# The first stage of a two-layer decoder step: input in nine loads, a padded short block, a bank of its own for the norms, and two column pairs side by side

## The chip, the cores and the metric

The kernel runs on one core of a Trainium2 chip. The metric is device time in microseconds (us). The kernel before was timed in three runs: 2272.81, 2275.51 and 2279.55, so its median is 2275.51 us. Engines are named as in the profile: PE is the matrix engine, PEld its weight loads, DVE the vector engine, ACT the scalar engine, POOL GpSimd, and SP the engine that issues most DMAs.

## What is computed

The program is one inference step of a decoder trunk with two layers: an RWKV-7 layer, then a sliding-window attention layer. All of the change lies at the start of the first layer. There the rows of the input are normalised, mixed with the row before, and multiplied by four weight matrices of 2048 x 4096:

```python
hp = concatenate([meta_tokens (16 rows), x_prompt (256 rows)])      # and x_sample: 8 rows
xn = hp * rsqrt(mean(hp * hp, axis=-1) + 1e-6) * a_norm             # D_MODEL = 2048
prev = concatenate([shift_prev, xn[:-1]])                           # state_shift for the samples
xm[p] = xn + (prev - xn) * mu[p]                                    # p = r, k, v, z, w, a
r, k, v, z = xm[p] @ w_rkvz[p]                                      # 2048 x 4096 each
```

The rest (the recurrence over the rows, the output projection and the attention layer) is not touched.

## The kernel before, in words

**Rows and blocks.** The 280 rows (16 meta tokens, 256 prompt rows, 8 samples) and the 8 rows of `state_shift` lie in three blocks `xt[0]`, `xt[1]`, `xt[2]` of 128, 128 and 32 rows by 2048 columns. They come in halves of 1024 columns. The loads of `xt[1]` and of the meta tokens are issued on ACT's queue, the others on SP's (lines 317 to 322). Each engine works through its queue in order, DMA issues included.

**Parameters.** `params` (line 251) is a generator. Its first part loads three small rows of parameters (`a_norm`, `a_mu`, `kv_norm`, lines 256 to 258, on ACT's queue), transposes them on PE into the PSUM bank `ps_par` (line 263) and copies them to `par` (line 264). Its second part does the same with two more blocks of rows, in the same bank.

**Norms.** The squares of each half and block are summed over the columns: block 0 on DVE (line 336), blocks 1 and 2 on ACT (line 334). Twelve small DVE instructions then make `rs`, the inverse root (lines 338, 339 and 299 to 303). Three transposes on PE spread `rs` over the partitions into the bank `ps_rs` (line 343), and ACT copies it to `rsb` (line 346). `ps_par` and `ps_rs` come from the pool `pp`, which has one bank.

**Transposes of the input.** For each of the 16 column blocks k (128 columns), PE transposes the three row blocks into one bank (line 362), and ACT copies the bank to `xn[:, k]` (line 364). The banks rotate over the pools `pe` (two banks), `pc` and `py` (one each). After every fourth k, `xn` is stored (line 366).

**Mixing.** For every group g of two column blocks, DVE multiplies by the norms (line 376), takes differences (lines 378, 379) and makes the mixed input `mst` (line 383). For the keys (m = 1) this runs for g = 0 to 7 in program order; the list of the results is `tk`. There are eight `mst` buffers.

**The keys' product.** `proj` (line 477) makes the result of a pair of 128 columns: it calls a product function, copies the two results (line 487), sums the squares of the keys (lines 490 and 493, bank `ps_kk`) and stores them. For the first two pairs the product function is `gemm32` (line 228): it multiplies in fp32, directly from `tk` and the raw weights. A raw tile holds two column blocks k by 256 columns (256 KB) and there are four such buffers (line 235). A pair needs eight raw tiles, and every fp32 product appears in the trace as two instructions (line 238). Its two result banks come from `pm`, which has three. Between the first and the second pair the program splits the mixed keys into two parts of lower precision, `xk` (cast on ACT, line 186; difference on DVE, line 187; store by SP, line 394), and does the same for five groups of the mixed values (`xv`).

All later products (the other fourteen pairs of the keys, and all of the values, receptance and gate) go through `gemm` (line 212): weights are split into `whi` and `wlo` (lines 186, 187), and each product is three PE instructions (lines 208 to 210). In the two pair-steps after the first two, groups of the mixed values and the mixed gate input are made and split beside the products; `behind` ties them to the weights' splits.

**What sets the order.** The program is written as a flow of data; a scheduler at build time orders the instructions of each engine. It takes them in program order, and lets later ones go first while earlier ones wait for data or buffers by its own estimate of times. Only the mixing for `tk` is bound by hand to its order on DVE.

Of the kernel before, what the change touches and what calls it, by code (L numbers as in the profile page):

```python
# [10 lines left out]
F32 = mybir.dt.float32  # L11
# [14 lines left out]
N = L + NS  # L26
NX = N + NS
NB = SEQ + NS
KT = D // 128
# [83 lines left out]
class Kernel:  # L113
# [113 lines left out]

    def gemm32(self, w, name, nk, col, x):

        ps = [self.bank(self.pm, f"ps_{name}_{col}_{c}") for c in (0, 128)]  # L230
        wv = w.rearrange("(kt p) c -> p kt c", p=128)
        for k0 in range(0, nk, 2):
            raw = self.wp.tile([128, 512], F32, tag="raw", bufs=4, name=f"raw_{name}_{col}_{k0}").rearrange(
                "p (k c) -> p k c", k=2)
            self.nc.sync.dma_start(raw, wv[:, k0:k0 + 2, col:col + 256])
            for i in range(2):
                for k in range(2):
                    self.nc.tensor.matmul(ps[i][:, :N], raw[:, k, 128 * i:128 * i + 128], x(k0 + k),
                                          start=k0 + k == 0, stop=k0 + k == nk - 1)
        return [p[:, :N] for p in ps]  # L240
# [10 lines left out]
    def params(self):  # L251
        nc, I = self.nc, self.I
        v = lambda n, k: I[n].rearrange("o (k c) -> (o k) c", c=128)
        rows = [self.ph.tile([128, 128], F32, name=f"prow{i}") for i in range(3)]

        nc.scalar.dma_start(rows[0][0:16], v('a_norm', 16))
        nc.scalar.dma_start(rows[0][16:112], I['a_mu'].rearrange("o m (k c) -> (o m k) c", c=128))
        nc.scalar.dma_start(rows[0][112:128], I['kv_norm'].rearrange("(k c) -> k c", c=128))
        self.par = self.cp.tile([128, 384], F32, name="par")
        ps = self.bank(self.pp, "ps_par")  # L260
        def par_of(i):
# [4 lines left out]
        yield  # L266
        dma = nc.sync.dma_start
        dma(self.ct[:, 128:], I['consts'][:, 128:C_TOTA])
# [40 lines left out]
    def phase0(self):  # L309
        nc, I, O, ph = self.nc, self.I, self.O, self.ph  # L310
        rows = [128, 128, 32]
        xt = [ph.tile([128, D], F32, name=f"xt{i}") for i in range(3)]
        xp = I['x_prompt'][0]
        dma = nc.sync.dma_start
        halves = slice(0, D // 2), slice(D // 2, D)
        for h in halves:
            nc.scalar.dma_start(xt[1][:, h], xp[112:240, h])
            dma(xt[0][16:128, h], xp[0:112, h])
            dma(xt[2][0:16, h], xp[240:256, h])
            dma(xt[2][16:24, h], I['x_sample'].rearrange("b o d -> (b o) d")[:, h])  # L320
            dma(xt[2][24:32, h], I['state_shift'][0, :, h])
            nc.scalar.dma_start(xt[0][0:16, h], I['meta_tokens'][:, h])
        params = self.params()
# [6 lines left out]
        for c, h in enumerate(halves):  # L330
            for i, r in enumerate(rows):
                sq = ph.tile([128, D // 2], F32, tag=f"sq{i % 2}", name=f"sq0_{i}{c}")[:r]
                if i:
                    nc.scalar.activation(sq, xt[i][:r, h], AF.Square, accum_out=sc[:r, c, i:i + 1])
                else:
                    nc.vector.tensor_tensor_reduce(sq, xt[i][:r, h], xt[i][:r, h], 1.0, 0.0, op0=ALU.mult,
                                                   op1=ALU.add, accum_out=sc[:r, c, i:i + 1])
# [3 lines left out]
        psr = self.bank(self.pp, "ps_rs")  # L341
        for i, r in enumerate((128, 128, 24)):
            nc.tensor.transpose(psr[:, i * 128:i * 128 + r], rs[:r, i:i + 1].to_broadcast((r, 128)),
                                self.ident[:r, :r])
        rsb = ph.tile([128, N], F32, name="rsb")
# [13 lines left out]
        for k in range(KT):  # L359
            ps = self.bank((self.pe, self.pc, self.pe, self.py)[k % 4], f"ps_xn{k}")  # L360
            for i, r in enumerate(rows):
                nc.tensor.transpose(ps[:, i * 128:i * 128 + r], xt[i][:r, k * 128:k * 128 + 128],
                                    self.ident[:r, :r])
            nc.scalar.copy(xn[:, k], ps[:, :NX])
            if k % 4 == 3:
                dma(self.xd[k - 3:k + 1].rearrange("k p t -> p k t"), xn[:, k - 3:k + 1, :N])
# [20 lines left out]
        def part(m, g, tile, t=None):  # L387

            if t is None:
                t = raw_part(m, g)  # L390
            hl = tile(f"d{m}_{g}")
            self.split(hl[:, 0], hl[:, 1], t)
            if m < 4:
                dma(self.md[m][g], hl.bitcast(F32))
            return hl
# [1374 lines left out]
```

## Time and profile before

| what | value |
|---|---|
| median of the three runs | 2275.51 us |
| span of the profiled execution | 2277.2 us |
| instructions | 57029 |
| bytes moved | 455.54 MB, mean 200 GB/s |
| first fp32 product of the keys (L238) | 28.98 us |
| first split product (L208) | 68.97 us |

The profile states the profiled execution's time as its span, from the first to the last instruction; the execution lies between the lowest and the highest of the three runs. All durations in the prediction are from this execution. The views used are: the page (busy time and share of each engine, the chain of work that ended last); busy time by windows (per engine, with the share of time in which the 16 DMA engines were busy, and GB/s); the chain of waits in order of time; the timeline, where each row gives start, length, engine, line and operation, output <- inputs, count, and in brackets the idle time before with what ended it; and groups of instructions, where the numbers are busy time, mean ns of one, and idle time before with what ended it.

### The profile page before, as it was taken

Reading aid. Unit: us, or ns where it says so; the run is one execution under the profiler, and the core shown is the slowest. Engines: PE = TensorE matmul, PEld = TensorE weight load, DVE = VectorE, ACT = ScalarE, POOL = GpSimd, SP = SyncE. Lnnn points to the kernel's source line nnn. Section 1 sums busy time; section 2 is a strip of 40 time slices with the busy share of each in tenths; the row PEclk is TensorE's granted clock in tenths of the full one; section 3 lists DMA queues with packets and bytes.
Section 4 is the critical chain, followed back from the end, with each engine's and each line's share of the span. In section 5 each row is a group of like instructions: output and inputs, shape, how many; then the busy total and the mean of one; then the engine's idle time right before and its main releaser. Section 6 shows DMA issues by size and latency. Waiting matters only on the chain.

```text
span 2277.2 us, 57029 instructions
## 1 busy us (share of the span) xinstructions
PE 2195.4 (96%) x21840; PEld 2029.5 (89%) x21840; DVE 1724.2 (76%) x4168; ACT 1303.8 (57%) x3074; POOL 60.7 (3%) x81
## 2 busy tenths in 40 slices
PE   6999999999999999999999999999999999999997
PEld 4898888899898889889889989999888899899997
DVE  5866756787787768788878878877767777787786
ACT  3556756576666567666665445644545544545443
POOL 0010000000000000000100001100000000000000
PEclk9999999999999999999999999999999999999998
DMA  7978667658755865766647677766434444367774
GB/s 241 340 255 249 185 198 241 194 174 266 227 163 179 247 230 177 246 206 200 201 129 265 192 236 245 227 201 191 134 104 127 133 144 133 105 194 218 232 230 145
DMA packets 424690, 455.54 MB, mean 200 GB/s; under 512 B 64201, under 2 KB 383113, under 8 KB 424025
## 3 DMA queue, kind: packets, MB, share of 16 engines
q1 hardware_dynamic: 423600, 449.61, 63.2%
q8 instruction: 171, 2.80, 0.5%
q10 hardware_dynamic: 816, 2.29, 0.3%
q14 instruction: 103, 0.84, 0.1%
HBM read 385.19 MB, written 70.73 MB: 200 GB/s over the span
## 4 chain that ended last, share of the span: by engine, by line
PE 80%; DMA 7%; DVE 6%; ACT 3%; issue 2%; SPq 0%; POOL 0%; DVEq 0%; ACTq 0%; POOLq 0%
PE ps_z L208 5%; PE ps_z L210 5%; PE ps_z L209 5%; PE ps_q L208 3%; PE ps_q L210 3%; PE ps_v L208 3%; PE ps_q L209 3%; PE ps_ob L210 3%; PE ps_k L208 3%; PE ps_ob L209 3%; PE ps_ob L208 3%; PE ps_v L209 2%; PE ps_v L210 2%; PE ps_k L209 2%; PE ps_k L210 2%; PE ps_r L208 2%
## 5 line engine op out<-in xcount | busy, mean ns | idle before, releaser
L187 DVE TENSOR_TENSOR wlo_z<-raw_z,whi_z 128x512 fp32r<-128x512 f32 x256 | 174.2, 689 | 61.7 <-ACT whi_z L186 54.7
L186 ACT CAST whi_z<-raw_z 128x512 fp32r<-128x512 f32 x256 | 155.8, 618 | 111.8 <-PE ps_z L209 67.9
L208 PE MATMUL ps_z<-mhlm,whi_z 128*128 128x280 f32 x512 | 159.1, 311 | 0.0
L210 PE MATMUL ps_z<-mhlm,wlo_z 128*128 128x280 f32 x512 | 150.3, 294 | 0.7 <-DVE wlo_z L187 0.6
L209 PE MATMUL ps_z<-mhlm,whi_z 128*128 128x280 f32 x512 | 150.0, 293 | 0.0
L208 PE MATMUL ps_q<-bmh,whi_q 128*128 128x264 f32 x512 | 148.5, 291 | 0.0
L208 PE MATMUL ps_z<-bmh,whi_z 128*128 128x264 f32 x512 | 147.4, 290 | 0.0
L209 PE MATMUL ps_q<-bml,whi_q 128*128 128x264 f32 x512 | 147.2, 289 | 0.0
L210 PE MATMUL ps_ob<-ghi,wlo_ob 128*128 128x264 f32 x512 | 145.3, 285 | 1.9 <-DVE wlo_ob L187 1.9
L209 PE MATMUL ps_z<-bml,whi_z 128*128 128x264 f32 x512 | 146.9, 289 | 0.0
L210 PE MATMUL ps_q<-bmh,wlo_q 128*128 128x264 f32 x512 | 146.5, 290 | 0.0
L210 PE MATMUL ps_z<-bmh,wlo_z 128*128 128x264 f32 x512 | 146.4, 289 | 0.0
L208 PE MATMUL ps_ob<-ghi,whi_ob 128*128 128x264 f32 x512 | 144.9, 284 | 0.0
L209 PE MATMUL ps_ob<-glo,whi_ob 128*128 128x264 f32 x512 | 144.7, 283 | 0.1
L187 DVE TENSOR_TENSOR wlo_r<-raw_r,whi_r 128x512 fp32r<-128x512 f32 x128 | 86.9, 686 | 57.2 <-ACT whi_r L186 56.1
L186 ACT CAST whi_oa<-raw_oa 128x512 fp32r<-128x512 f32 x128 | 78.4, 620 | 89.4 <-DMA raw_oa<-a_w_out 32.0
L186 ACT CAST whi_q<-raw_q 128x512 fp32r<-128x512 f32 x128 | 78.9, 621 | 81.6 <-PE ps_q L209 59.6
L187 DVE TENSOR_TENSOR wlo_v<-raw_v,whi_v 128x512 fp32r<-128x512 f32 x128 | 87.4, 688 | 49.5 <-ACT whi_v L186 43.6
L186 ACT CAST whi_ob<-raw_ob 128x512 fp32r<-128x512 f32 x128 | 78.9, 620 | 78.3 <-PE ps_ob L209 61.4
L208 PE MATMUL ps_v<-mhlm,whi_v 128*128 128x280 f32 x384 | 121.8, 317 | 0.2 <-ACT st L743 0.2
L208 PE MATMUL ps_k<-mhlm,whi_k 128*128 128x280 f32 x384 | 119.6, 312 | 0.0
L187 DVE TENSOR_TENSOR wlo_k<-raw_k,whi_k 128x512 fp32r<-128x512 f32 x112 | 76.5, 690 | 53.7 <-ACT whi_k L186 53.0
(486 smaller groups left out, 7686.0 us busy)
## 6 DMA issues: line engine op xcount, KB each, us to landing
raw_k<-a_w_rkvz SPq DMA_DIRECT2D x128, 256.0 KB
raw_v<-a_w_rkvz SPq DMA_DIRECT2D x128, 256.0 KB
raw_r<-a_w_rkvz SPq DMA_DIRECT2D x128, 256.0 KB
raw_z<-a_w_rkvz SPq DMA_DIRECT2D x128, 256.0 KB
raw_oa<-a_w_out SPq DMA_DIRECT2D x128, 256.0 KB
raw_q<-b_w_qz SPq DMA_DIRECT2D x128, 256.0 KB
raw_z<-b_w_qz SPq DMA_DIRECT2D x128, 256.0 KB
raw_ob<-b_w_o SPq DMA_DIRECT2D x128, 256.0 KB
```

Source lines behind the costliest of these rows:

```text
L186: self.nc.scalar.copy(hi, src)
L187: return self.nc.vector.tensor_tensor(lo, src, hi.bitcast(F32), op=ALU.subtract)
L208: mm(ps, wh, xh, start=start, stop=False)
L209: mm(ps, wh, xl, start=False, stop=False)
L210: return mm(ps, wl, xh, start=False, stop=stop)
```

## The change

Five things change, all at the start.

1. The input comes in eight loads, with the load of the constants nine: the meta tokens, the last prompt rows, the samples and `state_shift` come whole instead of in halves; `state_shift` goes to ACT's queue. The three first parameter rows go to SP's queue.
2. The short block `xt[2]` is padded: its rows 32 to 127 are set to zero by two fills on POOL, and its transposes, like the third one of the norms, are 128 x 128.
3. The squares of block 2 move from ACT to DVE.
4. `ps_par` moves to the pool `pc`, so `ps_rs` alone is in `pp` at that time. The transposes of the input now rotate over three banks (`pe`, `pe`, `py`).
5. `gemm32` takes both column pairs at once: per group of two column blocks it loads a raw tile for each pair and multiplies both; the four result banks come from `pm`, `pm`, `pc` and `pp`. The splits of `xk` and `xv` follow in the program after both pairs have been taken through `proj`.

```diff
-    def gemm32(self, w, name, nk, col, x):
+    def gemm32(self, w, name, nk, cols, x):
-        ps = [self.bank(self.pm, f"ps_{name}_{col}_{c}") for c in (0, 128)]
+        pools = self.pm, self.pm, self.pc, self.pp
+        ps = [self.bank(p, f"ps_{name}_{cols[i // 2]}_{i % 2}") for i, p in enumerate(pools)]
         wv = w.rearrange("(kt p) c -> p kt c", p=128)
         for k0 in range(0, nk, 2):
-            raw = self.wp.tile([128, 512], F32, tag="raw", bufs=4, name=f"raw_{name}_{col}_{k0}").rearrange(
-                "p (k c) -> p k c", k=2)
-            self.nc.sync.dma_start(raw, wv[:, k0:k0 + 2, col:col + 256])
-            for i in range(2):
+            for c, col in enumerate(cols):
+                raw = self.wp.tile([128, 512], F32, tag="raw", bufs=4, name=f"raw_{name}_{col}_{k0}").rearrange(
+                    "p (k c) -> p k c", k=2)
+                self.nc.sync.dma_start(raw, wv[:, k0:k0 + 2, col:col + 256])
                 for k in range(2):
-                    self.nc.tensor.matmul(ps[i][:, :N], raw[:, k, 128 * i:128 * i + 128], x(k0 + k),
-                                          start=k0 + k == 0, stop=k0 + k == nk - 1)
+                    for i in range(2):
+                        self.nc.tensor.matmul(ps[2 * c + i][:, :N], raw[:, k, 128 * i:128 * i + 128], x(k0 + k),
+                                              start=k0 + k == 0, stop=k0 + k == nk - 1)
...
-        nc.scalar.dma_start(rows[0][0:16], v('a_norm', 16))
-        nc.scalar.dma_start(rows[0][16:112], I['a_mu'].rearrange("o m (k c) -> (o m k) c", c=128))
-        nc.scalar.dma_start(rows[0][112:128], I['kv_norm'].rearrange("(k c) -> k c", c=128))
+        dma = nc.sync.dma_start
+        dma(rows[0][0:16], v('a_norm', 16))
+        dma(rows[0][16:112], I['a_mu'].rearrange("o m (k c) -> (o m k) c", c=128))
+        dma(rows[0][112:128], I['kv_norm'].rearrange("(k c) -> k c", c=128))
-        ps = self.bank(self.pp, "ps_par")
+        ps = self.bank(self.pc, "ps_par")
...
-        for h in halves:
-            nc.scalar.dma_start(xt[1][:, h], xp[112:240, h])
+        late = nc.scalar.dma_start
+        for c, h in enumerate(halves):
+            late(xt[1][:, h], xp[112:240, h])
             dma(xt[0][16:128, h], xp[0:112, h])
-            dma(xt[2][0:16, h], xp[240:256, h])
-            dma(xt[2][16:24, h], I['x_sample'].rearrange("b o d -> (b o) d")[:, h])
-            dma(xt[2][24:32, h], I['state_shift'][0, :, h])
-            nc.scalar.dma_start(xt[0][0:16, h], I['meta_tokens'][:, h])
+            if c == 0:
+                late(xt[0][0:16], I['meta_tokens'])
+                dma(xt[2][0:16], xp[240:256])
+        dma(xt[2][16:24], I['x_sample'].rearrange("b o d -> (b o) d"))
+        late(xt[2][24:32], I['state_shift'][0])
+        for r in (slice(32, 64), slice(64, 128)):
+            nc.gpsimd.memset(xt[2][r], 0.0)
...
-                if i:
+                if i == 1:
                     nc.scalar.activation(sq, xt[i][:r, h], AF.Square, accum_out=sc[:r, c, i:i + 1])
...
-            nc.tensor.transpose(psr[:, i * 128:i * 128 + r], rs[:r, i:i + 1].to_broadcast((r, 128)),
-                                self.ident[:r, :r])
+            nc.tensor.transpose(psr[:, i * 128:i * 128 + 128], rs[:, i:i + 1].to_broadcast((128, 128)), self.ident)
...
-            ps = self.bank((self.pe, self.pc, self.pe, self.py)[k % 4], f"ps_xn{k}")
+            ps = self.bank((self.pe, self.pe, self.py)[k % 3], f"ps_xn{k}")
-                nc.tensor.transpose(ps[:, i * 128:i * 128 + r], xt[i][:r, k * 128:k * 128 + 128],
-                                    self.ident[:r, :r])
+                nc.tensor.transpose(ps[:, i * 128:i * 128 + 128], xt[i][:, k * 128:k * 128 + 128], self.ident)
...
+        first = self.gemm32(I['a_w_rkvz'][0, 1], "k", KT, (0, 256), lambda k: tk[k // 2][:, k % 2])
         for p0 in (0, 2):
-            self.proj(1, lambda k: tk[k // 2][:, k % 2], [p0], self.kd, self.gemm32)
-            if p0 == 0:
-                xk = [part(1, g, self.mix_tile, tk[g]) for g in range(8)]
-                xv = [part(2, g, lambda nm: mv[g]) for g in range(5)]
+            self.proj(1, None, [p0], self.kd, lambda *_: first[p0:p0 + 2])
+        xk = [part(1, g, self.mix_tile, tk[g]) for g in range(8)]
+        xv = [part(2, g, lambda nm: mv[g]) for g in range(5)]
```

More of the change, by code (lines that the diff above doesn't have):

```diff
@@ L266, in params @@
         yield
-        dma = nc.sync.dma_start
         dma(self.ct[:, 128:], I['consts'][:, 128:C_TOTA])
@@ L310, in phase0 @@
         nc, I, O, ph = self.nc, self.I, self.O, self.ph
-        rows = [128, 128, 32]
         xt = [ph.tile([128, D], F32, name=f"xt{i}") for i in range(3)]
@@ L330, in phase0 @@
         for c, h in enumerate(halves):
-            for i, r in enumerate(rows):
+            for i, r in ((0, 128), (1, 128), (2, 32)):
                 sq = ph.tile([128, D // 2], F32, tag=f"sq{i % 2}", name=f"sq0_{i}{c}")[:r]
-                if i:
+                if i == 1:
                     nc.scalar.activation(sq, xt[i][:r, h], AF.Square, accum_out=sc[:r, c, i:i + 1])
@@ L341, in phase0 @@
         psr = self.bank(self.pp, "ps_rs")
-        for i, r in enumerate((128, 128, 24)):
-            nc.tensor.transpose(psr[:, i * 128:i * 128 + r], rs[:r, i:i + 1].to_broadcast((r, 128)),
-                                self.ident[:r, :r])
+        for i in range(3):
+            nc.tensor.transpose(psr[:, i * 128:i * 128 + 128], rs[:, i:i + 1].to_broadcast((128, 128)), self.ident)
         rsb = ph.tile([128, N], F32, name="rsb")
@@ L359, in phase0 @@
         for k in range(KT):
-            ps = self.bank((self.pe, self.pc, self.pe, self.py)[k % 4], f"ps_xn{k}")
-            for i, r in enumerate(rows):
-                nc.tensor.transpose(ps[:, i * 128:i * 128 + r], xt[i][:r, k * 128:k * 128 + 128],
-                                    self.ident[:r, :r])
+            ps = self.bank((self.pe, self.pe, self.py)[k % 3], f"ps_xn{k}")
+            for i in range(3):
+                nc.tensor.transpose(ps[:, i * 128:i * 128 + 128], xt[i][:, k * 128:k * 128 + 128], self.ident)
             nc.scalar.copy(xn[:, k], ps[:, :NX])
```

## The prediction

> **What bounds the kernel now.** The page is read first: its busy shares and the chain of work that ended last.
>
> ```profile
> PE 2195.4 (96%) x21840; PEld 2029.5 (89%) x21840; DVE 1724.2 (76%) x4168; ACT 1303.8 (57%) x3074; POOL 60.7 (3%) x81
> PE 80%; DMA 7%; DVE 6%; ACT 3%; issue 2%; SPq 0%; POOL 0%; DVEq 0%; ACTq 0%; POOLq 0%
> ```
>
> TensorE (PE) carries the kernel, so a change in the first stage is worth the time by which PE's later products move forward. The next view is busy time by stretches, cut where the first stage changes character.
>
> ```profile
> core 0: us, PE busy (x) PEld busy (x) DVE busy (x) ACT busy (x) POOL busy (x), PEclk, DMA share, GB/s
> 0.00:26.50 26.50, 14.66 (x54) 8.70 (x54) 4.60 (x21) 12.02 (x29) 1.18 (x8) 1.00 0.70 197
> 26.50:53.30 26.80, 20.25 (x71) 14.34 (x72) 25.67 (x57) 5.29 (x10) 0.00 (x0) 1.00 0.87 283
> 53.30:69.00 15.70, 15.45 (x63) 10.60 (x61) 8.12 (x17) 5.54 (x11) 0.00 (x0) 1.00 0.88 310
> 69.00:98.40 29.40, 29.14 (x205) 25.99 (x206) 27.36 (x53) 18.51 (x35) 0.00 (x0) 1.00 1.01 354
> 98.40:130.00 31.60, 31.60 (x214) 28.00 (x214) 27.08 (x61) 15.48 (x31) 0.00 (x0) 1.00 0.77 251
> ```
>
> Three regimes: until 26.5 a chain of loads, squares and transposes; until 53.3 DVE is full and PE waits for it; from 53.3 PE is full. From 69.0 to 98.4 PE, DVE and DMA are all nearly full at once; this will limit what the change is worth. The chain in order of time tells what ends last at the front (start, length, what):
>
> ```profile
> 5.40 5.75 DMA xt<-state_shift
> ...
> 11.91 2.19 ACT sq L334 x4
> ...
> 18.32 4.11 PE ps_xn L362 x15
> 22.43 0.40 PE ps_par L263
> 22.84 2.39 PE ps_xn L362 x9
> 25.23 0.86 PE ps_rs L343 x3
> 26.11 0.40 ACT rsb L346
> ```
>
> The transposes of the input hold PE, and the three transposes of the norms (`ps_rs`) come after the last of them, behind the last `ps_par`, whose bank they need. The timeline shows what that costs (start, length, engine, line, operation; in brackets the idle time before it and what ended it):
>
> ```profile
> 20.00 0.16 DVE L303 SCALAR_TENSOR_TENSOR rs<-rst,rsy 128x3 f32<-128x3 f32 x1
> 25.16 0.92 PE L343 MATMUL ps_rs<-consts,rs 128*128 128x128 f32 x3
> 26.54 0.93 DVE L376 SCALAR_TENSOR_TENSOR xn<-xn,par,rsb 128x280 f32<-128x280 f32 x2 [6.38 <-ACT rsb L346]
> 28.98 4.48 PE L238 MATMUL ps_k<-mst,raw_k 128*128 128x280 f32 x10 [2.91 <-DVE mst L383]
> 44.89 2.15 PE L238 MATMUL ps_k<-mst,raw_k 128*128 128x280 f32 x8 [1.03 <-DVE mst L383]
> 59.11 9.70 PE L238 MATMUL ps_k<-mst,raw_k 128*128 128x280 f32 x40
> 68.97 0.40 PE L208 MATMUL ps_k<-mhld,whi_k 128*128 128x280 f32 x1 [0.16 <-ACT whi_k L186]
> ```
>
> The norms are finished at 20.16 and used at 26.54: DVE idles 6.4 us. From 28.98 the first column pair takes eight PE instructions per group (two k tiles by two columns; each fp32 product shows as two instructions) and waits 1.03 for the next group. The second pair runs dense, and at 68.97 the split products begin.
>
> **The change, part by part.**
>
> *Input and parameters.* These rows of the timeline, of 2 us windows and of POOL's groups bear on it:
>
> ```profile
> 7.96 1.94 PE L362 MATMUL ps_xn<-consts,xt 128*128 128x128 f32 x8 [7.96 <-DMA xt<-x_prompt]
> 10.62 1.28 ACT L334 ACT_TABLE_LOAD   x1 [10.62 <-DMA prow<-a_mu]
> 14.13 1.23 DVE L336 CUSTOM_DVE_ANT_0 sq<-xt 128x1024 f32<-128x1024 f32 x1 [4.90 <-DMA prow<-a_a]
> 17.82 0.16 DVE L338 TENSOR_TENSOR rs<-ss 128x3 f32<-128x3 f32 x1 [2.46 <-ACT sq L334]
> 12.00:14.00 2.00, 0.45 (x1) 0.18 (x1) 0.00 (x0) 2.00 (x4) 0.00 (x0) 1.00 0.35 91
> L1428 POOL MEMSET Vm<- 32x1024 f32 x1 | 0.9, 945 | 0.0
> ```
>
> Four input issues go, and three parameter issues leave ACT's queue for SP's, past which the later parameters and weights then follow. The same bytes must arrive. The DMA share falls to 0.35 in 12 to 14, so the input is in at about 12.5 now, and I leave it there: the estimate runs from 11.5 (no gap in the stream) to 13.5 (the single loads of the short block arrive last and all columns need it). ACT loses its wait until 10.62 and the two squares of the short block; DVE gets those. Behind the landing DVE then has at most three squares, 3 x 1.31 = 3.9, and the norm chain of 2.34 (17.82 to 20.16): norms at 18.8. The parameters land behind the input, by about 14, and are used at 20: hidden; without that cover their cost is at most their delay. The two fills on POOL, about 1.9 each at 945 ns per 1024 columns, end near 5 and are hidden by the loading.
>
> *Padding.* Eight full transposes took 1.94, a pitch of 0.21. With the short block a column step lasts 0.86:
>
> ```profile
> 23.54 0.40 ACT L364 COPY xn<-ps_xn 128x288 f32<-128x288 f32 x1 [0.40 <-PE ps_xn L362]
> 24.05 0.53 PEld L362 LDWEIGHTS ps_xn<-consts,xt 32*128 32x128 f32 x3 [0.33 <-issue]
> 24.40 0.40 ACT L364 COPY xn<-ps_xn 128x288 f32<-128x288 f32 x1 [0.46 <-PE ps_xn L362]
> ```
>
> A short block stops the weight loads for 0.33, and the copies come 0.86 apart. Three full blocks at 0.21 take 0.64. From 12.5 on, some 42 of 48 remain: 9.0, and with three `ps_par` and three `ps_rs` 1.3 more: PE is through at 22.8. Copies of 0.40 fit inside 0.64, so three banks do as well as four. The Trainium skill, "TensorE: Matmul & The Clock Gate", section "LDWEIGHTS (loading the stationary operand)", speaks against this: a 32x128 load takes as long as a 128x128 one, so padding would save nothing on loads, while the moving side grows from 32 to 128 columns. The loads do agree (three short ones in 0.53), but the 0.33 ahead of them is in no such rule. No time in my sum rests on this.
>
> *Own bank for the norms.* `ps_rs` no longer waits for `ps_par`'s bank. With norms at 18.8, at most 0.6 until a column step ends, 0.95 (25.16 to 26.11) and 0.43 to DVE, DVE starts at about 20.5, 6.0 earlier. If the order leaves `ps_rs` last, it is 23.5. I take 20.5, since these transposes stand first in the program and only the bank held them. The first product follows 2.44 later (26.54 to 28.98) at 22.9, when PE is just through with the transposes.
>
> *Two pairs side by side.* Per group PE now has 16 instructions. Dense ones take 0.236 to 0.24 (x40 in 9.70), so a group takes 3.8, longer than DVE's spacing, which is 3.18 (two rows of the timeline, and the group of L238 with its idle time):
>
> ```profile
> 28.42 0.93 DVE L383 SCALAR_TENSOR_TENSOR mst<-dx,par,xn 128x280 f32<-128x280 f32 x2
> ...
> 31.60 0.93 DVE L383 SCALAR_TENSOR_TENSOR mst<-dx,par,xn 128x280 f32<-128x280 f32 x2
> L238 PE MATMUL ps_k<-mst,raw_k 128*128 128x280 f32 x128 | 34.7, 424 | 7.1 <-DVE mst L383 6.5 <-DMA raw_k<-a_w_rkvz 0.5
> ```
>
> So the waits for DVE go, and PE becomes the limit. All 128 instructions: the first 3.8 us slow at 0.45 (ten in 4.48), about 8 of them, then 120 x 0.24 = 28.8, and 1.0 for late weights: 33.6, ending at 56.5. The granted clock reads 1.00 throughout, so the slow start shows only in these durations. By the Trainium skill, same page, Part 1, PE starts slow and speeds up after a busy window of 3.4 us that does not start with the kernel; up to two windows slow would add an estimated 1.5 us. The ten slow rows agree as far as they go. The `ps_kk` work of the first pair (two stops of 0.57 between 54.95 and 59.11) moves behind, so today's comparable end is 68.97 - 1.1 = 67.9. Side by side ends 11.4 earlier: 6.0 from the front and 5.4 from the waits. Four banks are then emptied at once; PE goes on in the third `pm` bank meanwhile. What is late next is the weights, each a DMA of some 3.3 us (two pieces of the chain, and a row of SP's own waits: total, count, longest):
>
> ```profile
> 44.03 3.48 DMA raw_k<-a_w_rkvz
> 50.68 3.08 DMA raw_k<-a_w_rkvz
> SPq L394 <- DVE mhld L187: 14.4, 8, 2.3
> ```
>
> A buffer is free 1.9 after its turn and needed again 5.7 later, so 3.3 fits if SP issues within 2.4. Bounds: nothing late, up to 2.3 per group (SP's longest wait at a store).
>
> *What comes back.* The next two pairs find DMA full. Bytes until 98.4 are 26.5 x 197 + 26.8 x 283 + 15.7 x 310 + 29.4 x 354 = 28.1 MB (units of GB/s x us). After the change 2.6 MB are in by 14, some 1.6 MB follow until 22, and the rest, 23.9 MB at 354, takes 67.5: the pairs end at 89.5, not at 98.4 - 11.4 = 87.0. I give back 2.5. DVE's 61.2 us of work from 26.5 to 98.4 fit from 20.5 to 89.5. Between 98.4 and 130 the DMA share is only 0.77, so nothing more is lost there, and all later work hangs on these products.
>
> **Sum.** 6.0 + 5.4 - 2.5 = 8.9 us. The profiled span is 2277.2, 1.7 above the median of 2275.51 and inside the three runs (2272.81 to 2279.55): 2268.3 against the span, **2266.6** against the median. Its own range, from the landing (1 each way), late weights and the give-back (0 to 5), is 2263 to 2270.
>
> **The rivals.**
>
> *The full stretch takes more.* DMA and DVE are at 1.01 and 27.36 of 29.40 there. If stores of the split inputs crowd out weights, 6.5 comes back instead of 2.5: 2270.6. For it speaks that ACT already waits for `raw_k`; against, that PE has only 0.3 idle there.
>
> *Norms still last on PE.* DVE starts at 23.5, the front gives 3.0, less comes back (1.5): 6.9 gained, 2268.6.
>
> *Padding saves nothing*, the rule of the page named above. A step then keeps its 0.86 or, if a full block's 0.21 is added to it, grows to 1.07; at 0.96 instead of 0.64, 13 steps end some 4 us later, and the gain is 8.9 - 4 = 4.9: 2270.6. Against it stands the 0.21 of eight full blocks in a row.
>
> *It does not arrive.* A later wait swallows the lead: 2275. Against: PE is full from 98.4 to 130 and its later products wait for earlier ones.
>
> *Slower: SP's queue starves the side-by-side products.* Twice as many weights per group pass a queue that stands still 14.4 us at eight stores of split inputs, up to 2.3 each. If one of the two loads of each group stands behind such a store, PE waits there. With a lead of 8.9 over eight groups it decides from 1.1 us a group; at 2.0 a group it costs 16: 7 slower, 2282.5. For it: four buffers now hold only two groups. Against: the splits now come later in the program than the loads.
>
> **How the numbers follow.** Forecast 0.53; full stretch 0.12; norms last 0.10; padding 0.03; no arrival 0.08; slower 0.14. About 0.3%, 6.8 us, can be told from no change here. Beyond that faster are most of the forecast (0.49) and half of norms last (0.05): 0.54. Slower is the last case, 0.14. The rest, 0.32, is within. The range 2261 to 2279 leaves out the slow case and the edge of the forecast.
>
> **What the changed profile would show.** Right: `rsb` near 20, column steps 0.64 apart, the first L238 near 23 and the first L208 near 56, no DVE wait of 1.03 at L238, the values' first product near 89. Wrong: `ps_rs` behind the last `ps_xn`; L238 waiting for `raw_k` in most groups; a lead at 56 that has shrunk below 5 at 89; or a lead at 130 that is gone by the end.

## The result, and the profile after

The changed kernel took 2282.1 us in the median of 15 runs, the kernel before 2278.2 in 15 runs beside it; the ratio is 1.0013, with a 95% interval of 1.0002 to 1.0025. The forecast was 2266.6, with 2279 as the upper end of its range. A difference of 0.13% is no change by the bound of the prediction; the gain of 8.9 us did not come. One run of before here (2963.77) and one of best_again further down (2604.67) were disturbed, the latter at a granted clock of 0.751, and no ratio uses them.

The profiled execution of after is the second longest of its 15: 2287.3 us, span 2285.5. It is used for places and mechanisms, not for the size of the difference.

Below, the **lead** at a product is its start in the trace of before less its start in the trace at hand, so that a positive lead is time won. Between different executions a lead far behind the change also holds chance. An "fp32 product" is one of `gemm32` (L240 here, L238 before), a "split product" one of `gemm` (L208 to L210). The timeline of PE in after (start, length, engine, line, operation, idle time before and what ended it):

```profile
14.21 0.87 PE L366 MATMUL ps_xn<-consts,xt 128*128 128x128 f32 x3 [3.92 <-DMA xt<-x_sample]
15.15 2.18 PE L366 MATMUL ps_xn<-consts,xt 128*128 128x128 f32 x9
19.44 1.76 PE L366 MATMUL ps_xn<-consts,xt 128*128 128x128 f32 x12
21.04 0.49 PE L348 MATMUL ps_rs<-consts,rs 128*128 128x128 f32 x3
21.37 1.15 PE L366 MATMUL ps_xn<-consts,xt 128*128 128x128 f32 x9
24.44 7.81 PE L240 MATMUL ps_k<-mst,raw_k 128*128 128x280 f32 x32 [1.93 <-DVE mst L386]
35.51 7.78 PE L240 MATMUL ps_k<-mst,raw_k 128*128 128x280 f32 x32 [3.25 <-DMA raw_k<-a_w_rkvz]
43.45 15.33 PE L240 MATMUL ps_k<-mst,raw_k 128*128 128x280 f32 x64 [0.16 <-DMA raw_k<-a_w_rkvz]
58.41 0.50 PE L208 MATMUL ps_k<-mhld,whi_k 128*128 128x280 f32 x1
65.98 0.40 PE L208 MATMUL ps_k<-mhld,whi_k 128*128 128x280 f32 x1 [2.55 <-ACT whi_k L186]
69.46 0.60 PE L208 MATMUL ps_k<-mhld,whi_k 128*128 128x280 f32 x1 [1.30 <-ACT whi_k L186]
83.02 0.40 PE L208 MATMUL ps_k<-mhld,whi_k 128*128 128x280 f32 x1 [1.05 <-ACT whi_k L186]
83.88 0.40 PE L210 MATMUL ps_k<-mhld,wlo_k 128*128 128x280 f32 x1 [0.33 <-DVE wlo_k L187]
```

The norms (L348) now stand among the transposes, the fp32 products (L240) start at 24.44 instead of 28.98 and run without the 1.03 waits for DVE, and the split products begin at 58.41 instead of 68.97: a lead of 10.6. Then PE waits four times for weights, 5.2 us in all (the last four brackets); in the trace of before PE is idle for 0.3 from 69.0 to 98.4. Busy time by stretches in after shows the rest:

```profile
core 0: us, PE busy (x) PEld busy (x) DVE busy (x) ACT busy (x) POOL busy (x), PEclk, DMA share, GB/s
58.40:68.00 9.60, 7.05 (x42) 5.15 (x40) 4.15 (x8) 3.49 (x7) 0.00 (x0) 0.98 1.04 392
68.00:75.00 7.00, 5.70 (x26) 5.54 (x26) 4.97 (x9) 3.48 (x6) 0.00 (x0) 0.53 1.04 383
75.00:96.00 21.00, 19.62 (x135) 16.65 (x134) 17.52 (x35) 12.67 (x23) 0.00 (x0) 1.00 0.87 296
```

DMA is full until 75, and behind the waits the granted clock falls to 0.53 for 7 us, which costs 0.47 x 7 = 3.3. Together 8.5, against a lead that falls from 10.6 to 2.5 at the first product of the values (94.27; 96.80 in before). The chain of waits in after says which transfers these are (start, length, what; the first is the wait at 32):

```profile
29.30 6.07 DMA raw_k<-a_w_rkvz
...
55.03 5.13 DMA raw_k<-a_w_rkvz
...
62.23 6.53 DMA raw_k<-a_w_rkvz
```

In before the weights took 3.1 to 3.5 around 50, but nearly as long as here once its DMA was full, and PE did not wait for them. Its chain of waits:

```profile
67.33 4.49 DMA raw_k<-a_w_rkvz
...
72.58 5.68 DMA raw_k<-a_w_rkvz
```

So a long transfer alone does not stop PE. SP's timeline in after shows what else is late:

```profile
55.03 0.60 SPq L201 DMA_DIRECT2D raw_k<-a_w_rkvz  x1
55.73 3.33 SPq L397 DMA_DIRECT2D md<-mv  x3
59.16 1.16 SPq L201 DMA_DIRECT2D raw_k<-a_w_rkvz  x1
```

The load of 59.16 is the one behind the wait of 2.55. Side by side, PE frees a weight buffer every 1.9 us (eight products at 0.24), so a buffer for this load should be free about 1.9 after the one for the load at 55.03, near 57 (an estimate from these rows). SP issued three stores of split values first and came to the load some 2 us later.

At 165 the lead of this trace is 1.1, and by 1300 it has drifted to -1.2. At the output projection of the first layer, 1275 us behind the first product of the values, it steps from -1.1 to -6.7, that is 5.6 us lost in one place. PE, then DVE, in the timeline of after:

```profile
1369.36 0.29 PE L209 MATMUL ps_oa<-glo,whi_oa 128*128 128x280 f32 x1
1372.22 0.60 PE L210 MATMUL ps_oa<-ghi,wlo_oa 128*128 128x280 f32 x1 [2.57 <-DVE wlo_oa L187]
```

```profile
1369.68 1.53 DVE L1352 SCALAR_TENSOR_TENSOR gy<-gz,gy 128x280 f32<-128x280 f32 x4 [4.23 <-DMA gy<-yd]
...
1371.48 1.29 DVE L187 TENSOR_TENSOR wlo_oa<-raw_oa,whi_oa 128x512 fp32r<-128x512 f32 x2
```

The same place on DVE in before:

```profile
1363.56 0.68 DVE L187 TENSOR_TENSOR wlo_oa<-raw_oa,whi_oa 128x512 fp32r<-128x512 f32 x1
...
1364.52 0.68 DVE L187 TENSOR_TENSOR wlo_oa<-raw_oa,whi_oa 128x512 fp32r<-128x512 f32 x1
1368.08 1.53 DVE L1349 SCALAR_TENSOR_TENSOR gy<-gz,gy 128x280 f32<-128x280 f32 x4 [2.88 <-DMA gy<-yd]
```

In before the two weight splits that PE needs next stand ahead of the last gate `gy`, whose data is late anyway; in after they stand behind it, and DVE idles for 4.23 with them in its queue. The wait of PE is 2.57; the rest of the 5.6 is the clock again, which reads 0.51 from 1371.5 to 1378.5 (0.49 x 7 = 3.4). No line of this place was edited. The build-time scheduler draws the order of the whole program from its own estimate of times, so the edits of the first stage must have shifted that estimate.

So the theory to test is **two losses**: weights that come late on full DMA between 58 and 96, and a re-drawn order at 1369. Rivals: each of them is one execution's accident; or the lead would be lost whatever stands there.

### The profile page after: what moved, and what is told of

Its sections match the earlier page's. It is cut to its first block, busy times and chain, and to the rows that moved or that the text cites. A ratio compares the mean times of both kernels' runs of the same rounds, so it can differ in the third digit from the quotient of the medians.

```text
span 2285.5 us, 57031 instructions
## 1 busy us (share of the span) xinstructions
PE 2197.6 (96%) x21840; PEld 2039.0 (89%) x21840; DVE 1727.8 (76%) x4172; ACT 1304.6 (57%) x3070; POOL 64.1 (3%) x83
## 4 chain that ended last, share of the span: by engine, by line
PE 78%; DMA 9%; DVE 6%; ACT 4%; issue 2%; SPq 0%; DVEq 0%; ACTq 0%
PE ps_z L208 4%; PE ps_z L210 4%; PE ps_z L209 4%; PE ps_v L208 3%; PE ps_q L208 3%; PE ps_q L210 3%; PE ps_q L209 3%; PE ps_k L208 3%; PE ps_ob L210 3%; PE ps_ob L209 3%; PE ps_ob L208 3%; PE ps_v L209 3%; PE ps_v L210 3%; PE ps_k L210 2%; PE ps_k L209 2%
## 5 line engine op out<-in xcount | busy, mean ns | idle before, releaser
L186 ACT CAST whi_z<-raw_z 128x512 fp32r<-128x512 f32 x256 | 156.4, 619 | 105.0 <-PE ps_z L209 56.5
L208 PE MATMUL ps_z<-mhlm,whi_z 128*128 128x280 f32 x512 | 159.8, 312 | 0.0
L210 PE MATMUL ps_z<-mhlm,wlo_z 128*128 128x280 f32 x512 | 150.9, 295 | 0.5 <-DVE wlo_z L187 0.4
L208 PE MATMUL ps_q<-bmh,whi_q 128*128 128x264 f32 x512 | 148.3, 291 | 0.0
L210 PE MATMUL ps_ob<-ghi,wlo_ob 128*128 128x264 f32 x512 | 145.4, 285 | 1.9 <-DVE wlo_ob L187 1.9
L208 PE MATMUL ps_z<-bmh,whi_z 128*128 128x264 f32 x512 | 147.2, 289 | 0.0
L210 PE MATMUL ps_z<-bmh,wlo_z 128*128 128x264 f32 x512 | 146.7, 290 | 0.0
L210 PE MATMUL ps_q<-bmh,wlo_q 128*128 128x264 f32 x512 | 145.8, 290 | 0.0
L208 PE MATMUL ps_ob<-ghi,whi_ob 128*128 128x264 f32 x512 | 144.9, 284 | 0.0
L208 PE MATMUL ps_v<-mhlm,whi_v 128*128 128x280 f32 x384 | 122.5, 319 | 0.3 <-ACT whi_v L186 0.3
L208 PE MATMUL ps_k<-mhlm,whi_k 128*128 128x280 f32 x384 | 120.1, 313 | 0.0
```

What stands on the lines that cost most here:

```text
L186: self.nc.scalar.copy(hi, src)
L208: mm(ps, wh, xh, start=start, stop=False)
L210: return mm(ps, wl, xh, start=False, stop=stop)
```

## The experiments

The kernel before ran beside each of the three sets of experiments: 2279.2, 2279.0 and 2278.5 us in the median of 35, 35 and 29 runs. Each experiment has 12 timed runs. An interval is some 0.25% wide, 6 us, so most single ratios here cannot be told from 1; the verdicts rest on the traces and on pairs of runs. "First V" is the start of the first product of the values (L208 on `ps_v`), 96.80 in before. PE's order around it differs a little between kernels: counted product by product, a lead there is up to 1.6 us less or 1.0 more than First V says.

| kernel | median us | ratio to before | 95% interval | first V |
|---|---|---|---|---|
| after_again | 2281.6 | 1.0010 | .9997 to 1.0024 | 92.29 |
| front_only | 2276.6 | 0.9989 | .9973 to 1.0004 | 92.76 |
| side_only | 2280.5 | 1.0010 | .9994 to 1.0025 | 96.50 |
| late_stores | 2285.0 | 1.0027 | 1.0015 to 1.0039 | 87.98 |
| after_order | 2279.2 | 1.0003 | .9990 to 1.0016 | 95.86 |
| front_gy_ahead | 2278.9 | 1.0003 | .9990 to 1.0016 | 95.41 |
| order_lw | 2275.4 | 0.9989 | .9977 to 1.0000 | 93.66 |
| order_lw_hold | 2275.2 | 0.9988 | .9976 to 1.0000 | 87.76 |
| best_again | 2278.1 | 0.9993 | .9981 to 1.0005 | 92.37 |
| order_lw_hold8 | 2276.9 | 1.0000 | .9988 to 1.0012 | 85.07 |
| front_unpadded | 2280.0 | 1.0008 | .9998 to 1.0018 | 97.66 |

**after_again**: after, not edited.

> The changed kernel once more, for a second profile. In its first profile PE led the kernel before by 10.0 us between 50 and 75 and by 1.0 from 100 on; PE stood still 2.84 and 1.74 at 63 and 68 for weights, and the granted clock was halved from 67.7 to 74.5. A step of 5.6 followed at 1369. Theory (late weights): the two waits between 60 and 70 and the halved clock come again, lead at 117 between 0 and 3. The step at 1369 does not come again; the time is then about 2280. Rival (chance): no halved clock near 68, lead at 117 of 4 or more. Second rival (the change costs time late in the kernel): the step at 1369 comes again.

Both places came again: idle times of PE of 2.5, 0.65 and 1.05 us from 62.5 to 81, and at 1369 a loss of 4.5 (the lead goes from 3.7 to -0.75). Neither is an accident of one execution.

**front_only**: after, with `gemm32` and the order of `xk` and `xv` of before.

```diff
-        first = self.gemm32(I['a_w_rkvz'][0, 1], "k", KT, (0, 256), lambda k: tk[k // 2][:, k % 2])
...
-            self.proj(1, None, [p0], self.kd, lambda *_: first[p0:p0 + 2])
+            self.proj(1, lambda k: tk[k // 2][:, k % 2], [p0], self.kd, self.gemm32)
...
```

> Loads, padding and bank of the changed kernel, with the two column pairs one after the other as before. Theory (late weights): the first fp32 product comes at 24.4 as in the changed kernel, DVE is again the limit of the first pair, the fp32 products end near 64; PE then runs into the same full stretch of DMA, but later, with waits of 1 to 2 in all; lead at 117 of 2 to 4; time 2 to 4 below the kernel before. Rival (the lead is lost whatever its source): lead at 117 of 1 or less, time as before.

The lead is 4.6 at the first product, 3.6 at 50 and 4.0 from there to 165. PE waits 1.03 per group as in before, and from 58 to 96 it has no wait above 0.3, though the DMA share from 58 to 75 is 1.03, as in after. The median is 2.7 us under before, not quite outside its noise: if any part pays, it is the front.

**side_only**: before, with the new `gemm32` and the new order alone.

> The kernel before with the two column pairs side by side and nothing else of the change. Theory (late weights): the first fp32 product comes at 29 as before, the fp32 products end near 63 to 64 (33 to 34 of dense work, with one wait for weights of about 3 as in the changed kernel perhaps more); the splits are then late and stores crowd the weights from 62 on; waits of 3 to 5; lead at 117 of 0 to 2, time within 2 of before. Rival (side by side as such is good): lead at 117 of 5.

The lead of 7.9 at the first split product (61.07) is 0.3 at the first product of the values. In its timeline PE waits twice for weights:

```profile
28.58 32.85 PE L240 MATMUL ps_k<-mst,raw_k 128*128 128x280 f32 x128 [2.91 <-DVE mst L385]
68.12 0.40 PE L208 MATMUL ps_k<-mhld,whi_k 128*128 128x280 f32 x1 [2.08 <-ACT whi_k L186]
72.20 0.40 PE L208 MATMUL ps_k<-mhld,whi_k 128*128 128x280 f32 x1 [2.06 <-ACT whi_k L186]
```

All that the pairs side by side win is handed back within 36 us.

**late_stores**: after, with 13 stores of split inputs (all eight of the keys, five of the values) held and issued beside the values' products.

```diff
+            if m == 1 or m == 2 and g < 5:
+                held.append((m, g, hl))
-            if m < 4:
+            elif m < 4:
...
+            for i in range(min(4, len(held))):
+                m, g, hl = held.pop(0)
+                with self.tc.issue_after(self.raws[2 * i - 8].ins):
+                    dma(self.md[m][g], hl.bitcast(F32))
```

> The changed kernel with the 13 stores of the split keys' input (8) and of the first five groups of the values' input (7.3 MB) held back and issued beside the values' products, one behind every second load of weights. Everything is computed. Theory (late weights from full DMA and stores ahead of loads): no wait of PE over 1 between 55 and 75, no halved clock there, lead at 117 of 7 to 9, and it lasts: 2270 to 2273, 6 to 8 below the kernel before. Rival A (DVE is the limit in that stretch): waits move to the lower weight parts, lead at 117 of 2 to 4. Rival B (the lead does not arrive at the end): lead at 117 of 7 or more, time as the kernel before or above.

The lead holds: about 10 at 85, 8.8 at the first product of the values. So the stores do take it away. DMA keeps a share of 0.94 from 58 to 75 (1.03 in after); what has changed most is that the weights are ahead of the stores. But these come due later, and windows of this kernel show where:

```profile
96.00:130.00 34.00, 34.00 (x228) 30.17 (x227) 22.91 (x52) 13.57 (x28) 0.00 (x0) 1.00 0.97 333
130.00:165.00 35.00, 31.27 (x212) 28.99 (x211) 21.30 (x39) 16.91 (x37) 6.11 (x10) 0.95 0.89 303
```

DMA goes from 0.75 in after to 0.97, PE loses 3.7 us from 130 to 165, and at 225 the kernel is 4.4 behind before. Of the kernels in the table it is the only one whose interval lies above 1.

**after_order**: after, with the last gate made behind the two weight splits, as in before.

```diff
...
+        with self.tc.issue_after(self.los[-4].ins):
+            for pl in range(4):
+                self.nc.vector.scalar_tensor_tensor(y[:, pl], z[:, pl], 0.5, y[:, pl], op0=ALU.mult, op1=ALU.mult)
...
```

> After, with one thing put back: in the output product near 1369 us VectorE forms the last gate (gy) behind the split of the ninth and tenth weight tiles, as in before, not ahead of the fourth group's splits. Theory A (a part of the missing gain is lost at 1369, because the program's order on VectorE came out differently there): TensorE's gap of 2.9 us at 1369 goes back to under 1, the lead there no longer jumps by 3.6 to 5.6 us, and the median falls from 2281.6 to about 2277.5 (ratio to before .9975 to 1.000). Rival (the gate's transfer is late whatever the order, so that TensorE only waits some instructions later): 2281 as after, ratio 1.001, with a gap of 2 to 3 us by 1375.

No gap at 1369, and the gate does not hold up the splits. DVE in its timeline:

```profile
1364.33 0.68 DVE L187 TENSOR_TENSOR wlo_oa<-raw_oa,whi_oa 128x512 fp32r<-128x512 f32 x1
1367.94 1.53 DVE L1381 SCALAR_TENSOR_TENSOR gy<-gz,gy 128x280 f32<-128x280 f32 x4 [2.93 <-DMA gy<-yd]
```

The median is 2.4 us lower than after_again's (1.6 by the ratios, as the two ran in different sets): the right sign, and less than the 4 expected.

**front_gy_ahead**: front_only, with the splits put behind the gate.

```diff
+            if (name, col, k0) == ("oa", 0, 6) and nk == KE - 4 * G1 and self.gy7:
+                with self.tc.issue_after(self.gy7.ins):
+                    self.los.append(self.split(hi, lo, raw))
...
```

> The kernel with the front part alone (2276.6, ratio .9989, where this order is as in before), with the fourth group's low halves put behind the last gate on VectorE, which is after's order near 1369 us. Theory A: TensorE waits 2.5 to 3 us there, and the median rises by 3 to 5 us, to 2280 (ratio 1.0005). Rival (the order costs nothing): 2276.6 and .999 again.

The wait appears where there was none (timeline of PE):

```profile
1375.20 0.40 PE L214 MATMUL ps_oa<-ghi,wlo_oa 128*128 128x280 f32 x1 [2.16 <-DVE wlo_oa L187]
```

The median rises by 2.3 (3.2 by the ratios). Taken away from the one kernel and put into the other, the order is worth 2.4 and 2.3 us. Neither difference stands out of its noise alone, some 3 us each way; they have the right sign both times, and the wait itself is shown both ways.

**order_lw**: after_order, with the loads of the low-rank weights queued behind the 16th split weight load.

```diff
-                    dma(raw, wv[:, k0:k0 + 4])
+                    with self.tc.issue_after(self.raws[15].ins):
+                        dma(raw, wv[:, k0:k0 + 4])
```

> After with the order at 1369 put back, and with the low-rank weights' loads queued behind the 16th of the split weight loads, so that they no longer stand ahead of the raw weights of the third and fourth group of the side-by-side products. Theory (the wait of 3.2 us at 32 is SP's order; what is won before 58 is lost again at 62 to 84 to weights that come late on full DMA): first split product at 55 instead of 58.4, the first product of the values at 94 all the same, and the time that of the kernel with the order alone, within 1 us. Rival (every us won before 58 lasts): first product of the values near 91, 3 us faster than with the order alone.

The 3.25 wait at 32 is gone and the 128 products run through. PE's timeline in this kernel:

```profile
23.97 32.14 PE L240 MATMUL ps_k<-mst,raw_k 128*128 128x280 f32 x128 [1.96 <-DVE mst L386]
55.74 0.50 PE L208 MATMUL ps_k<-mhld,whi_k 128*128 128x280 f32 x1
...
67.57 0.60 PE L208 MATMUL ps_k<-mhld,whi_k 128*128 128x280 f32 x1 [5.31 <-ACT whi_k L186]
```

55.74 is what the forecast wanted (56.5), and one wait of 5.3 with a clock of 0.91 from 57 to 96 (0.09 x 39 = 3.5) takes it back: the lead is 13 at 56 and 3.1 at the first product of the values, no more than after_again's 4.5. SP's rows say why the wait grew: the load that ends it is issued at 60.65, 6.4 behind the load before it (54.26), with four stores of split values and two of results in between. By place the theory is right. By time the rival is nearer: the median is 3.8 under that of after_order, just outside the noise of the two. Part of this may be the clock: in after_order's trace it was 0.82 from 57 to 96.

**order_lw_hold**: the same, and five of the thirteen stores held.

```diff
+            if m == 2 and g < 5:
+                held.append((m, g, hl))
...
+            for i in range(min(2, len(held))):
+                m, g, hl = held.pop(0)
+                with self.tc.issue_after(self.raws[4 * i - 8].ins):
+                    dma(self.md[m][g], hl.bitcast(F32))
```

> The kernel before this one, and the stores of the first five mixed parts of the values (five of the thirteen that run in the full stretch) held and issued beside the values' products, where DMA shares of .75 to .8 leave room. Theory (bytes in the stretch from 58 to 96 take the lead away; thirteen moved stores gave 8.8 us at the first product of the values, but filled the next stretch to .96): a lead of 5 to 7 us at the first product of the values, DMA share from 96 to 130 at about .87, at least 3 us of it kept at 230, and 2273 to 2275 (ratio .998). Rival (the whole of the first 230 us is bound by DMA, so that the lead goes wherever the stores stand): lead gone by 230, 2277 or more.

```profile
57.00:96.00 39.00, 36.46 (x241) 30.65 (x240) 31.10 (x61) 21.71 (x40) 0.00 (x0) 1.00 1.01 352
96.00:130.00 34.00, 34.00 (x231) 30.44 (x230) 26.17 (x60) 14.14 (x31) 0.00 (x0) 1.00 0.83 277
```

No wait for weights above 1 us is left, the clock stays at 1.00, and DMA has room from 96 on. Before that it is full (1.01); what is gone is the stores between the loads, and SP issues four weight loads between 56.2 and 58.3. The lead is 9.0 at the first product of the values, 8.3 at 225, 11 at the end: this execution has a span of 2266.4 and is the shortest of its twelve. The median of twelve is 2275.2.

**best_again**: the same kernel once more.

> The kernel with the order put back, the low-rank weights behind and five stores held, once more as it is. Theory: its lead of 8 to 11 us over before from 96 us to the end is its own and comes again in this trace, and the ratio is .998 to .9995. Rival (the lead after 500 us was one execution's luck, in which TensorE's clock was halved less often): the lead at 100 is 8 to 9 again, but 4 or less at 1800.

```profile
57.00:96.00 39.00, 36.12 (x223) 30.80 (x223) 29.48 (x58) 21.23 (x40) 0.00 (x0) 0.91 0.96 335
```

The rival was right. Here one idle time of PE, before `ps_kk` at 79.69, was 1.94 us instead of 1.17, the clock fell, the lead is 4.4 at the first product of the values, 2.7 at 225 and 0.3 at the end (span 2277.0). So a lead of 8 to 11 is not this kernel's own; what it keeps in the medians of its two sets is 3.9 and 0.4 us, and both intervals reach 1.

**order_lw_hold8**: eight stores held (`m == 1 and g > 4` too), three beside each of the first two pairs and two beside the third.

> As the kernel before, with eight stores held (the last three mixed parts of the keys too), three, three and two beside a pair of the values' products. Theory (each byte moved out of 58 to 96 is kept until the next stretch is full): lead at the first product of the values 8 to 9 instead of 6.5 to 7, DMA share from 96 to 130 at .9, and at 230 the lead is 7 to 9, so the time is that of five stores within 1.5 us. Rival (as with thirteen stores, the stretch from 130 to 225 takes it all back): lead under 3 at 230, and 2279 or more.

The first product of the values is 11.7 ahead (10.2 counted product by product), DMA is at 0.95 from 96 to 130, and the lead is 5.9 at 225 and 6.6 at the end of this trace, again the shortest of its twelve. The median, 2276.9, is 1.7 under before and within noise of it. The theory is the nearer one: more is kept until 96 than expected (8 to 9), less at 225 (7 to 9), and the time is within 1.3 us of best_again's from the same set.

**front_unpadded**: front_only, with the short block's transposes as in before.

```diff
...
-            for i in range(3):
-                nc.tensor.transpose(ps[:, i * 128:i * 128 + 128], xt[i][:, k * 128:k * 128 + 128], self.ident)
+            for i, r in enumerate((128, 128, 32)):
+                nc.tensor.transpose(ps[:, i * 128:i * 128 + r], xt[i][:r, k * 128:k * 128 + 128], self.ident[:r, :r])
```

> The kernel with the front part alone, but with the short block's transposes as in before (32 rows, 32 x 32 identity, no zero fill), the other edits of the front kept. Theory (full transposes both save the stall in each column and bring TensorE to full speed ahead of the first product): the columns take .8 to .86 again where they aren't waiting for input, the first product comes at 24.5 to 26, the first products run .45 apart until some 8 us after it, and of the lead of 4.0 us at 50 only 0 to 2 is left; 2278 to 2279, ratio .9995 to 1.0005. Rival (the front's gain comes from the order of the loads and the norms' place alone): first product at 24, lead of 4 at 50, 2276.5, ratio .999.

```profile
14.91 2.60 PE L362 MATMUL ps_xn<-consts,xt 128*128 128x128 f32 x9
...
20.47 5.18 PE L362 MATMUL ps_xn<-consts,xt 128*128 128x128 f32 x18
25.58 0.90 PE L344 MATMUL ps_rs<-consts,rs 128*128 128x128 f32 x3
26.27 0.88 PE L362 MATMUL ps_xn<-consts,xt 128*128 128x128 f32 x3
29.39 8.54 PE L238 MATMUL ps_k<-mst,raw_k 128*128 128x280 f32 x24 [2.24 <-DVE mst L382]
```

A column takes 0.86 again, the first product comes at 29.39 and starts slowly (24 in 8.54), and the lead at 50 is -0.7. Padding was expected to carry two to four of the front's 4.0 us; it carries all of them, and the median is 3.4 us above that of front_only. The DVE row of this kernel shows how:

```profile
26.95 0.93 DVE L375 SCALAR_TENSOR_TENSOR xn<-xn,par,rsb 128x280 f32<-128x280 f32 x2 [6.63 <-ACT rsb L346]
```

The norms are finished at 20.32, as early as in front_only (20.82), and `ps_rs` has its own bank. But PE's order has it behind 15 of the 16 columns, and at 0.86 a column that is 25.58: DVE waits for it as long as it did in before.

## Why the prediction was wrong, point by point

*Input and norms: right in kind, 4.5 instead of 6.0.* The short block's last loads held the columns back until 14.21 (12.5 was taken, with 13.5 as the latest), so DVE started at 22.00 and the products at 24.44 (22.9 was taken).

*Own bank for the norms: wrong as the cause.* The 6.0 was put down to the bank, and no time in the sum was to rest on padding. In front_unpadded the bank is there and DVE starts at 26.95, no earlier than in before (26.54). In after `ps_rs` stands behind 13 of the 16 columns, and comes at 21.04 because the columns are fast. So without padding the other edits of the front gain nothing here; whether padding would have done it without the bank was not tried.

*Padding: right, and worth more than stated.* Columns took 0.72 at first (9 in 2.18), then 0.44 (12 in 1.76). With and without it the same kernel differs by 4.3 us at 50. The rule weighed in the prediction (the Trainium skill, "TensorE: Matmul & The Clock Gate", section "LDWEIGHTS (loading the stationary operand)") speaks of the load's own time, and that is not what padding saved; the rival drawn from it, that padding saves nothing, was wrong. The slow start of the products that the prediction counted was gone too in this trace: PE was at full speed before them.

*Side by side: right but for the weights.* The fp32 products ran at 0.24 without a wait for DVE, but the two loads of the third group's weights cost 3.25 where 1.0 was allowed for all late weights. SP's timeline in after:

```profile
23.52 2.21 SPq L410 DMA_DIRECT2D lw<-a_w  x2
25.84 0.57 SPq L369 DMA_DIRECT2D xd<-xn  x1
26.45 2.05 SPq L410 DMA_DIRECT2D lw<-a_w  x2
28.59 0.61 SPq L397 DMA_DIRECT2D md<-mhld  x1
29.30 1.34 SPq L237 DMA_DIRECT2D raw_k<-a_w_rkvz  x2
```

And in order_lw, without the four low-rank loads ahead:

```profile
28.79 1.32 SPq L237 DMA_DIRECT2D raw_k<-a_w_rkvz  x2
```

The issue itself comes only 0.5 later in after; but it then took 6.07 to land, by the chain above, with the low-rank bytes on the queues. So at this wait SP's order, as the expectation for order_lw had it, was the smaller part, and the bytes ahead the larger. Without them the split products began at 55.74. The rival in which SP's queue starves every group of the fp32 products was wrong: of eight groups one was late by more than 0.2.

***What comes back* is the step that failed.** It gave back 2.5 us, worked out from bytes at an even 354 GB/s, with the pairs ending at 89.5; the 3.3 us that the prediction took for a load were from around 50, while its own trace has 4.49 and 5.68 in the full stretch. The trace of after gave back some 8: 5.2 in waits for single weight loads and 3.3 in a halved clock behind them. An even flow of bytes has no waits; PE needs each tile at its time, and here a stop of 2.55 was followed by half speed for 7 us. That moved stores keep the lead through this stretch (late_stores, order_lw_hold) shows that the stores of the split inputs are the cause; order_lw shows that an earlier arrival at 56 only lengthens the wait. Whether they act by their bytes or by their places ahead of the loads in SP's queue no run tells apart, as holding them takes away both. The rows speak for the places: from 58 to 75 DMA is as good as full in after (1.03) and just so in front_only (1.03) and order_lw_hold (1.01), where PE hardly waits, and the loads that end the long waits of after and order_lw were issued 4.1 and 6.4 behind the load before them. So two rivals were nearer than the forecast: "the full stretch takes more" had 6.5 coming back because stores crowd out weights, and "SP's queue starves" had the mechanism, but looked for it one step too early.

*"Nothing more is lost there, and all later work hangs on these products" failed too.* From 96 to 165 it held (the lead of after stays near 1 in its trace). But the queues' orders far behind the change were drawn anew, and at 1369 this cost 2.3 to 2.4 us in the medians. Two of the signs named for a wrong prediction came: a lead below 5 at 89 (about 1.5), and a lead at 130 (1.2) that is gone by the end (-8.2).

The sum in medians, roughly: the front gains 2.7 (front_only), the pairs side by side lose 1.3 (side_only), the order at 1369 costs 2.4, so after should be 1.0 slower; it was 3.9 and, in after_again, 2.4. The rest isn't told apart from noise, and that the parts add up is not shown either, since each has a noise of some 3 us. What stays open is why little of a lead of 3 to 8 us at 225 arrives in the medians; the last section says what the runs show of it.

## What to carry to other kernels

Do not cost a stage that is full on several resources at once by its bytes alone: ask when each tile is needed, when its load is issued and when it lands. Look for stores that stand between the loads and can leave the stage before work is moved into it, with the next stage's room as the limit. Where a scheduler orders the program at build time, compare the order of each engine's queue far behind an edit as well; a late operand at the head of an in-order queue is paid by all behind it. A short block that breaks an engine's pitch can be worth padding; test it alone, as here the gain had been put down to another edit.

## What the runs showed of the hardware

Short gaps cost more than themselves. Over the 13 traces, from 30 to 2200 us, there are 29 gaps of 2.5 to 3.0 us from the start of one product of PE to the next; in 22 cases the granted clock fell to 0.5, for 3.4 us or a multiple of it, by 2 us after the gap. Behind gaps of 0.9 to 1.4 us it did in 10 of 151. Whether a gap is hit differs between executions: order_lw_hold and best_again, the same kernel, read 1.00 and 0.91 from 57 to 96; and PE's idle time ahead of `ps_kk` was 1.85 us in order_lw_hold8 and 1.94 in best_again, and only the second was followed by a lower clock. The Trainium skill, "TensorE: Matmul & The Clock Gate", Part 1, says that the activity window is free-running, so that the same kernel differs from run to run; the traces agree with that.

The spread of the runs goes with this clock. The twelve runs of order_lw_hold spread over 14.5 us (2268.2 to 2282.7); the shortest had a mean granted clock of 0.989, the longest 0.985. In every kernel here longer runs have the lower clock, with 1.1 to 1.9 us for each 0.001. It also differs between kernels: in the second and third set the runs of before had 0.9887 in the mean and those of the five kernels with the pairs side by side 0.9859 to 0.9872 (front_gy_ahead 0.9882, front_unpadded 0.9901). By that slope the difference is worth 2 to 5 us, an estimate, and of the size of the lead that does not arrive. That it is all of it was not tried.

Full-size fp32 transposes can bring PE to full speed: in after nine of them took 2.18 us from 15.15 on, and twelve took 1.76 from 19.44 on. In six of the ten traces with padding the first 32 fp32 products ran at full pitch at once (7.81 in after); in the other four a halved clock of 3.4 us fell on them (32 in 9.50 in after_again). In the three traces without padding they always started slowly.
